# The first mixer of a two-block transformer kernel: products of the next heads traced in steps of six between steps of scores

## The chip, the cores and the metric

The kernel runs on one core of one Trainium2 chip. The metric is the device time of one execution in microseconds (us). The engines are named as in the profile: PE (TensorE's matmuls), PEld (its weight loads), DVE (VectorE), ACT (ScalarE), POOL (GpSimd) and SP (SyncE, which issues most DMAs).

## The reference, cut to what matters

The program computes two blocks one after the other. The change lies in the first layer of block 2, in the mixer that stands ahead of that layer's feed-forward part. It works on 512 tokens of `x` and 256 context tokens, 768 in all, each 1024 wide:

```python
def mixer_ab(hx, hc, w_in, w_out, sink, lam_vec, subln_g, lam_init, tab, ctx_queries):
    p = hx @ w_in                                   # q, k, v of both kinds of heads
    ...                                             # axial rotary embedding of qa, ka, qb, kb
    pc = hc @ w_in
    ...
    oa = window_gqa_latent(qa, ka, va, cka, cva, sink)          # 8 heads, window and context
    ob = from_blocks(lax.map(lambda qblk: diff_attend(qblk, [(kb, vb), (ckb, cvb)], lam),
                             to_blocks(qb)))                     # 4 heads, two softmaxes each
    yx = jnp.concatenate([oa, diff_out(ob, subln_g, lam_init)], axis=-1) @ w_out
    ...                                             # the same for the 256 context tokens

def diff_attend(q, kv_parts, lam):
    ...
    outs = [jnp.einsum('bhqk,bkhd->bqhd', (p[:, 0] - lam * p[:, 1]).astype(v.dtype), v)
            for p, (_, v) in zip(probs, kv_parts)]
```

The windowed heads see their neighbouring tiles of 128 keys and the context. A differential head takes two softmaxes over all 768 keys and subtracts the second, scaled by `lam`, from the first.

## The kernel before, in words

All large products are done as three matmuls each (`mm3`, lines L207 to L209): an operand is split in a high and a low part, and high by high, high by low and low by high are summed in PSUM. A product of one weight tile of 128 columns with the 768 tokens ("load" of q, k or of a pair of windowed queries) is 24 matmuls of 512 columns and 24 of 256. It then goes through `rope_sink`: ACT copies it out of PSUM (L1280), DVE, POOL and DVE rotate it (L1281 to L1284), ACT and DVE write its halves (L1286, L1287, for the last 256 tokens L259 and L260), and `queries` or `keys` move halves between partitions by DMAs issued by SP (L1306). ACT also writes a twin of one half (L1277, L1289). A load of v (`values`, L1470 on) has three sets of 48 matmuls of 256 columns.

In `mixer0` two kinds of units follow each other. Wa, Wb, Wc with a number are the three parts (token tiles 0 and 1, 2 and 3, context) of a pair of windowed heads; Dx and Dc with a number are the two parts (four token tiles, two context tiles) of a differential head. A unit has a generator of scores and one of weighing. The scores of a Dx tile are two rows of 512 and 256 columns (`scores_64`, L1333 and L1334), one for each softmax, each in one of the two PSUM buffers "s2". DVE takes the maximum (L1504), ACT the exponentials and their sum (L1506), DVE its reciprocal (L1507), POOL scales the first (L1510), and DVE joins the two (L1512). Weighing transposes the probabilities by matmuls with the identity (L1347 for D, L700 for W), splits them into halves (ACT L256 and DVE L257, for W L703 and L705) and multiplies them with the values; the D units then normalise with two more transposes (L1533 to L1548).

`unit` weaves the scores of a unit with the weighing of the unit before it, one step by one. The order of units and loads is the table `SEQ`. A load in it is traced whole, between two units; a "." finishes the weighing of the unit before at that point. From the trace a list scheduler makes each engine's order, so the order of instructions is near to that of the program, and not the same. PSUM has eight banks: two buffers "t" (transposes), two "s2" of two banks, one "o" (weighing), one "g" (loads; head 0's q and k use "t").

Of the kernel before, what the change touches and what calls it, by code (L numbers as in the profile page):

```python
# [1363 lines left out]
class Win:  # L1364
# [91 lines left out]
class Diff:  # L1456
# [4 lines left out]
    def load(self, hF, win, h, what, tag="g"):  # L1461

        K, P = self.K, self.P
        c, scale = (512, 0.125) if what == "q" else (1280, 1.0)
        s = (Halves(K, P, P.t("ds", [128, 768], K_DS, F32R)) if what == "q" else
             Halves(K, P, P.t("kl", [128, 768], 1, F32R), P.t("kl1", [128, 768], 1, F32R)))
        gemm_F(K, hF, win[:, :, c:c + 512], 768, lambda j, o, p: s.sink(P, scale)(o, p), [h], tag=tag)
        self.qk[what, h] = s.queries() if what == "q" else s.keys()

    def values(self, hF, win, h, order=(0, 2, 4), early=False):  # L1470
# [595 lines left out]
def hF_tile(P, n=768):  # L2066
# [1 line left out]


STEP = 1.0  # L2070
SEQ = ("k0 Wq0 q0 Wa0 Dx0 Dc0 q1 k1 Wb0 Dx1 Dc1 Wc0 Wq1 Wa1 q2 k2 Wb1 v2 Dx2 . Wc1 Wq2 Dc2 . Wa2 q3 Wb2 k3 Wc2 Dx3 . Wq3 Wa3 Wb3 "
       "Wc3 Dc3")
CTX_FIRST = (4, 5, 0, 1, 2, 3)
PARTS = ((512, 768), (0, 256), (256, 512))

# [1 line left out]
def mixer0(K, hF, finish):  # L2077
# [6 lines left out]
    with ExitStack() as es:  # L2084
# [54 lines left out]
        def diff(h, tiles):
            unit("diff", lambda probs: df.scores(h, tiles, probs), lambda probs: df.weigh(h, tiles, probs), 4 + h if tiles[0] else None)  # L2140

        def qk(h, *what):
            for x in what:
                if x == "v":
                    run_all(df.values(hF, win, h))
                else:
                    df.load(hF, win, h, x, "g" if h else "t")

        for what in SEQ.split():
            if what == ".":  # L2150
                weigh_last()
                continue
            x, h = what[:-1], int(what[-1])
            if x == "Wq":
                W.load_q(hF, win, h)
            elif x in ("Wa", "Wb", "Wc"):
                units = units if x > "Wa" else list(W.units(h))
                unit("win", *units["abc".index(x[1])], h if x == "Wc" else None)
            elif x in ("Dx", "Dc"):
                diff(h, (0, 1, 2, 3) if x == "Dx" else (4, 5))  # L2160
# [171 lines left out]
```

## Time and profile before

| | us |
|---|---|
| median of three runs | 2549.37 |
| lowest and highest | 2546.64 to 2550.6 |
| profiled execution | 2548.71 |
| its span | 2546.7 |
| mean granted clock of PE, share of full speed | 0.982 |
| the mixer of the change in the span | some 850 to 1164 |

Busy time is the time in which an engine has an instruction under way; matmuls overlap in the records, so PE at 100% in a window is a continuous stream. In a timeline a row has its start, its length, the engine, the line and the operation, and in brackets the idle time ahead of it with the instruction that ended it. Places are named by their time in the span.

### The profile page before, as it was taken

How to read it: one execution, taken by the hardware profiler on the slowest of the kernel's cores; microseconds unless marked ns; L12 is line 12 of the kernel's file. 1: busy time of each engine (PE TensorE's matmuls, PEld its weight loads, DVE VectorE, ACT ScalarE, POOL GpSimd, SP SyncE). 2: the span in 40 equal slices, each digit the busy share in tenths (PEclk: the TensorE clock that was granted, in tenths of full speed). 3: DMA queues.
4: the chain of work that ended last, by engine and by line, in shares of the span. 5: the costliest groups of instructions: out<-in, count | busy, mean ns of one | idle time of the engine just before them, and what ended most of it. 6: DMA issues, size and time to landing. Idle time of an engine off the chain costs nothing. (4 is left out here: it accounts for less than half of the span.)

```text
span 2546.7 us, 37857 instructions
## 1 busy us (share of the span) xinstructions
PE 2417.0 (95%) x15436; PEld 1980.4 (78%) x15436; DVE 1199.3 (47%) x2075; ACT 996.9 (39%) x1802; POOL 303.4 (12%) x393
## 2 busy tenths in 40 slices
PE   8999989999999988989899999999899999999998
PEld 6567758788887867768888888888777768888886
DVE  5654474433446575763532223233756564423344
ACT  4642244432325454553522211212555564432222
POOL 1101132000001122220200000000232222000001
PEclk9999989999999999989999999999999999999999
DMA  8765475333334312122411222222331124333332
GB/s 271 243 199 170 162 262 178 92 99 91 99 100 148 85 51 60 50 90 83 150 58 59 66 67 62 64 83 62 109 74 35 40 67 126 106 99 99 93 106 91
DMA packets 251005, 270.74 MB, mean 106 GB/s; under 512 B 23744, under 2 KB 198256, under 8 KB 244688
## 3 DMA queue, kind: packets, MB, share of 16 engines
q1 hardware_dynamic: 249600, 264.00, 33.6%
q0 software_dynamic: 1232, 4.33, 0.5%
q8 instruction: 121, 1.98, 0.3%
q14 instruction: 52, 0.43, 0.1%
HBM read 231.90 MB, written 25.45 MB: 101 GB/s over the span
## 5 line engine op out<-in xcount | busy, mean ns | idle before, releaser
L207 PE MATMUL ps<-hFh,wh 128*128 128x512 f32 (+1 forms) x1752 | 629.0, 360 | 11.0 <-ACT qk_l L1277 3.5
L208 PE MATMUL ps<-hFl,wh 128*128 128x512 f32 (+1 forms) x1752 | 625.0, 357 | 1.5 <-DVE hFl L266 1.3
L200 DVE TENSOR_TENSOR wl<-wr,wh 128x1024 fp32r<-128x1024 f32 (+3 forms) x258 | 307.3, 1192 | 672.5 <-ACT wh L199 655.4
L209 PE MATMUL ps<-hFh,wl 128*128 128x512 f32 (+1 forms) x1752 | 623.5, 356 | 0.5 <-DVE wl L200 0.5
L199 ACT CAST wh<-wr 128x1024 fp32r<-128x1024 f32 (+3 forms) x258 | 263.2, 1021 | 711.9 <-PE ps L208 350.5
L207 PEld LDWEIGHTS ps<-hFh,wh 128*128 128x128 f32 x1752 | 332.7, 190 | 76.4 <-issue 14.5
L209 PEld LDWEIGHTS ps<-hFh,wl 128*128 128x128 f32 x1752 | 333.0, 190 | 53.5 <-issue 5.6
L208 PEld LDWEIGHTS ps<-hFl,wh 128*128 128x128 f32 x1752 | 333.5, 190 | 48.9 <-DVE hFl L266 3.1
L207 PE MATMUL ps<-wh,h_h 128*128 128x512 f32 x590 | 229.7, 389 | 0.7 <-ACT wh L199 0.7
L208 PE MATMUL ps<-wl,h_h 128*128 128x512 f32 x590 | 229.7, 389 | 0.0
L209 PE MATMUL ps<-wh,h_l 128*128 128x512 f32 x590 | 229.5, 389 | 0.0
L1827 POOL TENSOR_TENSOR yg<-y,gainrow 128x512 f32<-128x512 f32 x28 | 38.7, 1384 | 1316.2 <-DVE y L1119 866.5
L207 PEld LDWEIGHTS ps<-wh,h_h 128*128 128x128 f32 x590 | 110.8, 188 | 24.0 <-ACT wh L199 1.1
L208 PEld LDWEIGHTS ps<-wl,h_h 128*128 128x128 f32 x590 | 110.8, 188 | 23.0 <-DVE wl L200 0.2
L209 PEld LDWEIGHTS ps<-wh,h_l 128*128 128x128 f32 x590 | 110.8, 188 | 23.0
L1238 DVE TENSOR_TENSOR hraw<-hraw,ps 128x512 f32<-128x512 f32 (+1 forms) x70 | 40.1, 573 | 176.0 <-PE ps L209 176.0
L1628 DVE TENSOR_REDUCE sm<-ps 128x1 f32<-128x768 f32 x64 | 60.9, 952 | 49.3 <-PE ps L209 48.6
L265 ACT CAST h_h<-hraw 128x512 fp32r<-128x512 f32 (+1 forms) x70 | 36.9, 527 | 120.4 <-DVE hraw L1238 120.4
L207 PE MATMUL ps<-wh,hFh 128*128 128x256 f32 (+2 forms) x256 | 80.3, 315 | 1.2 <-DVE qk_l L257 1.2
L208 PE MATMUL ps<-wl,hFh 128*128 128x256 f32 (+2 forms) x256 | 80.2, 313 | 0.2 <-DVE wl L200 0.2
L209 PE MATMUL ps<-wh,hFl 128*128 128x256 f32 (+2 forms) x256 | 80.2, 313 | 0.0
L1632 POOL TENSOR_SCALAR ms<-ms,sm 128x768 f32<-128x768 f32 x64 | 62.0, 970 | 149.1 <-DVE sm L1631 145.6
(643 smaller groups left out, 4174.8 us busy)
## 6 DMA issues: line engine op xcount, KB each, us to landing
wr<-in_ffn_w_dram SPq DMA_DIRECT2D x126, 512.0 KB, 3.8
aw<-in_ada_w_dram SPq DMA_DIRECT2D x48, 1024.0 KB, 5.1
wr<-in_mlp_w_dram SPq DMA_DIRECT2D x60, 512.0 KB, 3.9
wr<-in_w_in_dram SPq DMA_DIRECT2D x25, 512.0 KB, 6.1
x<-xr SPq DMA_DIRECT2D x20, 512.0 KB, 2.8
xr<-x SPq DMA_DIRECT2D x18, 512.0 KB, 3.7
wr<-in_ab_w_in_dram SPq DMA_DIRECT2D x16, 512.0 KB, 4.3
wr<-in_w_out_dram SPq DMA_DIRECT2D x8, 512.0 KB, 4.5
```

Source lines behind the costliest of these rows:

```text
L199: nc.scalar.copy(dst(hi), view(raw))
L200: nc.vector.tensor_tensor(out=dst(lo), in0=view(raw), in1=dst(hi).bitcast(F32), op=SUB)
L207: mm(out, a.hi, b.hi, start=start, stop=False)
L208: mm(out, a.hi, b.lo, start=False, stop=False)
L209: mm(out, a.lo, b.hi, start=False, stop=stop)
L265: nc.scalar.copy(s.hi, x)
L1238: v.tensor_tensor(out=raw[:, c], in0=raw[:, c], in1=p, op=MUL)
L1628: v.tensor_reduce(out=mx, in_=p[:, 0:768], axis=AX.X, op=MAX, negate=True)
L1632: nc.gpsimd.tensor_scalar(out=s, in0=s, scalar1=r, scalar2=1.0, op0=MUL, op1=MUL)
L1827: nc.gpsimd.tensor_tensor(out=t[:, h[0]], in0=y[:, h[0]], in1=g[:, h[0]], op=MUL)
```

## The change: what it does

The loads become generators. `load_steps` yields after every six matmuls (eight steps for a load), `values` after every twelve. One background generator, `loading`, runs through the loads in the order of `LOADS`; `weave` advances it by `SHARES` steps at each score step of a unit (one in the W units, two in D, three in Wb2 and Wc2). `ready` runs what is still missing ahead of a unit that needs it. The units have a regular order, three W and two D for each number. The points at which a weighing was finished early are gone, and all loads use the bank "g".

The core of the diff (left out: the empty lines, and the code that reads the tables):

```diff
+def load_steps(K, act, src, sink, tag):
+
+    w = K.weight(src)
+    for o, e in ((0, 512), (512, 768)):
+        p = K.ps(tag)[:, 0:e - o]
+        for k in range(8):
+            K.mm3(p, w[:, k], act[:, k, o:e], k == 0, k == 7)
+            if k % 2 and k < 7:
+                yield
+        sink(o, p)
+        if not o:
+            yield
...
-        gemm_F(K, hF, win[:, :, c:c + 512], 768, lambda j, o, p: s.sink(P, scale)(o, p), [h], tag=tag)
+        yield from load_steps(K, hF, win[:, :, c + 128 * h:c + 128 * h + 128], s.sink(P, scale), tag)
...
-SEQ = ("k0 Wq0 q0 Wa0 Dx0 Dc0 q1 k1 Wb0 Dx1 Dc1 Wc0 Wq1 Wa1 q2 k2 Wb1 v2 Dx2 . Wc1 Wq2 Dc2 . Wa2 q3 Wb2 k3 Wc2 Dx3 . Wq3 Wa3 Wb3 "
-       "Wc3 Dc3")
+SHARES = {"Wa": 1, "Wb": 1, "Wc": 1, "Dx": 2, "Dc": 2, "Wb2": 3, "Wc2": 3}
+UNITS = ("Wa0 Wb0 Wc0 Dx0 Dc0 Wa1 Wb1 Wc1 Dx1 Dc1 Wa2 Wb2 Wc2 Dx2 Dc2 Wa3 Wb3 Wc3 Dx3 Dc3").split()
+LOADS = ("Wq0 q0 k0 Wq1 q1 k1 Wq2 q2 v2 k2 Wq3 q3 k3").split()
+NEEDS = {"W": ("Wq",), "D": ("q", "k", "v")}
...
+        def loading():
+            while loads:
+                yield from loads[0][1]
+                loads.pop(0)
+                yield
...
         def unit(name, scores, weigh, sent=None):
             probs = []
-            weave(marked(K, name, scores(probs)), (going[0] if going else iter(()), STEP))
+            weave(marked(K, name, scores(probs)), (going[0] if going else iter(()), STEP), (bg, SHARES.get(name, SHARES[name[:-1]])))
             weigh_last()
```

The instructions are the same in number on PE; they move. Three places show it on PE. In these rows a name is followed by its number in the program; the changed kernel's lines L1347, L1348, L1361, L714 and L728 are L1333, L1334, L1347, L700 and L714 of the kernel before.

The first place is the mixer's first scores. Of the kernel before, the end of the third load and the first rows of Wa0's scores (ps_7985 and ps_7999); ps_7955 is the second part of that load:

```order
L207 MATMUL ps_7955<-hFh_6980,wh_7916 128x256
L208 MATMUL ps_7955<-hFl_6981,wh_7916 128x256
L209 MATMUL ps_7955<-hFh_6980,wl_7917 128x256
L1333 MATMUL ps_7985<-qk_h_7323,qk_h_7838 128x256
L1334 MATMUL ps_7985<-qk_h_7321,qk_h_7838 128x256
L1333 MATMUL ps_7985<-qk_h_7323,qk_h_7838 128x256
L1334 MATMUL ps_7985<-qk_h_7321,qk_h_7838 128x256
L1333 MATMUL ps_7999<-qk_h_7323,qk_h_7838 128x256
L1334 MATMUL ps_7999<-qk_h_7321,qk_h_7838 128x256
```

Of the changed kernel, the last of the ten matmuls of q0's load (ps_7856) that follow the load Wq0, and the first scores:

```order
L207 MATMUL ps_7856<-hFh_6980,wh_7852 128x512
L208 MATMUL ps_7856<-hFl_6981,wh_7852 128x512
L209 MATMUL ps_7856<-hFh_6980,wl_7853 128x512
L207 MATMUL ps_7856<-hFh_6980,wh_7852 128x512
L1347 MATMUL ps_7833<-qk_h_7323,qk_h_7760 128x256
L1348 MATMUL ps_7833<-qk_h_7321,qk_h_7760 128x256
L1347 MATMUL ps_7833<-qk_h_7323,qk_h_7760 128x256
L1348 MATMUL ps_7833<-qk_h_7321,qk_h_7760 128x256
L1347 MATMUL ps_7863<-qk_h_7323,qk_h_7760 128x256
```

Before, three whole loads stand ahead of the first scores; now one load and ten matmuls of the second.

The second place is Dx0. Of the kernel before, two rows of its scores (ps_8104 and ps_8115) and what lies between them: matmuls of the next load (ps_8333), of Wa0's values (ps_8066) and a transpose:

```order
L1333 MATMUL ps_8104<-qk_h_7761,qk_h_7912 128x512
L1334 MATMUL ps_8104<-kl_7759,qk_h_7912 128x512
L1333 MATMUL ps_8104<-qk_h_7761,qk_h_7912 128x256
L1334 MATMUL ps_8104<-kl_7759,qk_h_7912 128x256
L714 MATMUL ps_8066<-pt_h_8173,wv_7337 64x256 x2
L209 MATMUL ps_8333<-hFh_6980,wl_8330 128x512
L1347 MATMUL ps_8210<-c_ident,pr_8049 128x128
L207 MATMUL ps_8333<-hFh_6980,wh_8329 128x512
L1333 MATMUL ps_8115<-qk_l_7762,qk_l_7913 128x512
L1334 MATMUL ps_8115<-kl_1269_7760,qk_l_7913 128x512
L1333 MATMUL ps_8115<-qk_l_7762,qk_l_7913 128x256
L1334 MATMUL ps_8115<-kl_1269_7760,qk_l_7913 128x256
```

Of the changed kernel, three rows of the same scores (ps_8236, ps_8291, ps_8302) and the first of the next (ps_8349):

```order
L1348 MATMUL ps_8236<-kl_8085,qk_h_7848 128x512
L1347 MATMUL ps_8236<-qk_h_8087,qk_h_7848 128x256
L1348 MATMUL ps_8236<-kl_8085,qk_h_7848 128x256
L1347 MATMUL ps_8291<-qk_h_8087,qk_h_7848 128x512
L1348 MATMUL ps_8291<-kl_8085,qk_h_7848 128x512
L1347 MATMUL ps_8291<-qk_h_8087,qk_h_7848 128x256
L1348 MATMUL ps_8291<-kl_8085,qk_h_7848 128x256
L1347 MATMUL ps_8302<-qk_l_8088,qk_l_7849 128x512
L1348 MATMUL ps_8302<-kl_1340_8086,qk_l_7849 128x512
L1347 MATMUL ps_8302<-qk_l_8088,qk_l_7849 128x256
L1348 MATMUL ps_8302<-kl_1340_8086,qk_l_7849 128x256
L1347 MATMUL ps_8349<-qk_h_8087,qk_h_7848 128x512
```

Between these rows no matmul of a load or of a weighing stands any more; the next load's first four (ps_8475) follow two and a half rows later.

The third place is the end of Dx3's scores. Of the kernel before, the start of Dx3's weighing (ps_10495 and ps_10507 transposes, ps_10494 the product with the values) and Wa3's scores (ps_10662, ps_10676) within it:

```order
L1347 MATMUL ps_10495<-c_ident,pr_10475 128x128
L1347 MATMUL ps_10507<-c_ident,pr_10475 128x128
L207 MATMUL ps_10494<-pt_h_10500,qk_h_9337 128x512
L1333 MATMUL ps_10662<-qk_l_7324,qk_h_10589 128x256
L1334 MATMUL ps_10662<-qk_l_7322,qk_h_10589 128x256
L1333 MATMUL ps_10662<-qk_l_7324,qk_h_10589 128x256
L1334 MATMUL ps_10662<-qk_l_7322,qk_h_10589 128x256
L1333 MATMUL ps_10676<-qk_l_7324,qk_h_10589 128x256
L1334 MATMUL ps_10676<-qk_l_7322,qk_h_10589 128x256
L1333 MATMUL ps_10676<-qk_l_7324,qk_h_10589 128x384
L1334 MATMUL ps_10676<-qk_l_7322,qk_h_10589 128x384
L208 MATMUL ps_10494<-pt_l_10501,qk_h_9337 128x512
```

Of the changed kernel, the last scores of Dc3 (ps_10895, ps_10904) and Dx3's weighing (transposes ps_10883, ps_10916, ps_10928, product ps_10882):

```order
L1347 MATMUL ps_10895<-qk_h_10418,qk_h_10119 128x256
L1348 MATMUL ps_10895<-kl_10416,qk_h_10119 128x256
L1347 MATMUL ps_10904<-qk_l_10419,qk_l_10120 128x256
L1348 MATMUL ps_10904<-kl_1883_10417,qk_l_10120 128x256
L1361 MATMUL ps_10883<-c_ident,pr_10821 128x128
L1361 MATMUL ps_10916<-c_ident,pr_10821 128x128
L207 MATMUL ps_10882<-pt_h_10888,qk_h_9523 128x512
L208 MATMUL ps_10882<-pt_l_10889,qk_h_9523 128x512
L209 MATMUL ps_10882<-pt_h_10888,qk_l_9524 128x512
L207 MATMUL ps_10882<-pt_h_10921,qk_h_9523 128x512
L1361 MATMUL ps_10928<-c_ident,pr_10726 128x128
L1361 MATMUL ps_10928<-c_ident,pr_10759 128x128
```

Dx3 and Dc3 are the last units now: behind these scores only Dx3's and Dc3's weighing stands ahead of the output product. The last load (k3) ends within the scores of Wc3.

## Rows read from the trace of the kernel before

**Rows 1.** The page: busy time of the engines; shares of the chain of waits.
```profile
PE 2417.0 (95%) x15436; PEld 1980.4 (78%) x15436; DVE 1199.3 (47%) x2075; ACT 996.9 (39%) x1802; POOL 303.4 (12%) x393
...
PE 22%; DVE 3%; issue 1%; ACT 1%; DMA 1%; POOL 1%; DVEq 0%; POOLq 0%; ACTq 0%
```

**Rows 2.** Windows: us, PE, PEld, DVE, ACT, POOL busy, PEclk, DMA share, GB/s.
```profile
885.00:925.00 40.00, 37.47 (x216) 30.00 (x215) 30.85 (x70) 24.35 (x52) 11.52 (x17) 0.96 0.13 38
940.00:980.00 40.00, 33.17 (x179) 25.36 (x178) 28.77 (x74) 21.54 (x50) 12.12 (x25) 0.91 0.09 24
1036.00:1076.00 40.00, 36.95 (x224) 29.99 (x223) 31.30 (x86) 23.98 (x55) 15.36 (x30) 1.00 0.18 57
1100.00:1140.00 40.00, 31.28 (x172) 23.94 (x169) 30.93 (x62) 24.15 (x47) 10.27 (x20) 0.87 0.34 112
1157.67:1163.59 5.92, 3.75 (x26) 2.17 (x23) 3.75 (x9) 3.39 (x9) 0.60 (x2) 1.00 0.00 0
1300.00:1350.00 50.00, 50.00 (x290) 44.25 (x289) 13.74 (x18) 11.72 (x18) 0.00 (x0) 1.00 0.21 64
```

**Rows 3.** Waits of PE, 850 to 1165 us: sum, times, longest, all us.
```profile
PE ps L1347 <- DVE pr L1512: 8.2, 5, 3.3
PE ps L1547 <- DVE pt_h L1544: 4.3, 6, 1.1
PE ps L207 <- ACT qk_l L1277: 3.5, 6, 1.1
PE ps L207 <- DVE qk_l L257: 2.1, 3, 1.0
```

**Rows 4.** Timelines, head 0: start us, length us, engine, line, [idle before <-releaser].
```profile
858.29 0.39 PE L209 MATMUL ps<-hFh,wl 128*128 128x512 f32 x1
858.52 0.28 PE L207 MATMUL ps<-hFh,wh 128*128 128x256 f32 x1
864.46 0.42 DVE L260 SCALAR_TENSOR_TENSOR kl<-ps,qk_h 128x256 fp32r<-128x256 f32 x1 [0.37 <-ACT qk_h L259]
880.34 0.35 PE L1333 MATMUL ps<-qk_h,qk_h 128*128 128x256 f32 x1 [1.88 <-ACT qk_h L1286]
```

**Rows 5.** DMA issues, 840 to 1170 us: times, KB, median us to landing.
```profile
qk_h<-ds SPq DMA_DIRECT2D x8, 192.0 KB, 2.8
```

**Rows 6.** Lines by form, 850 to 1165 us: busy us, mean ns, idle before.
```profile
L1504 DVE TENSOR_REDUCE sm<-ps 128x1 f32<-128x768 f32 x32 | 30.2, 949 | 7.7 <-PE ps L1334 7.5
L1512 DVE SCALAR_TENSOR_TENSOR pr<-ds,sm,pr 128x768 f32<-128x768 f32 x16 | 16.3, 1018 | 0.3 <-POOL pr L1510 0.2
L1506 ACT ACTIVATE ds<-ps,sm 128x768 f32<-128x768 f32 x16 | 14.5, 904 | 1.8 <-DVE sm L1504 1.3 <-DVE sm L1507 0.2 <-issue 0.2
L256 ACT CAST pt_h<-ps 128x512 fp32r<-128x512 f32 x28 | 15.8, 587 | 15.9 <-PE ps L1347 15.8
L257 DVE TENSOR_TENSOR pt_l<-ps,pt_h 128x512 fp32r<-128x512 f32 x28 | 18.6, 686 | 6.9 <-ACT pt_h L256 6.8
```

**Rows 7.** Timeline of PE, a row of Dx1's scores.
```profile
953.15 0.50 PE L1333 MATMUL ps<-qk_h,qk_h 128*128 128x512 f32 x1 [1.22 <-ACT pr L1506]
```

**Rows 8.** Timeline of PE, end of Dx3's scores, and Dx3's weighing.
```profile
1125.07 0.69 PE L1347 MATMUL ps<-c_ident,pr 128*128 128x128 f32 x2 [3.33 <-DVE pr L1512]
1130.36 1.04 PE L1347 MATMUL ps<-c_ident,pr 128*128 128x128 f32 x8
```

**Rows 9.** Timelines of ACT and PE, Dx3's weighing and the mixer's end.
```profile
1137.20 0.59 ACT L1533 COPY pt_h<-ps 128x512 f32<-128x512 f32 x1 [0.98 <-PE ps L209]
1143.82 0.67 ACT L1548 ACTIVATE mo<-ps,sub 128x512 f32<-128x512 f32 x1
1157.39 0.28 PE L1334 MATMUL ps<-kl,qk_l 128*128 128x256 f32 x1
1158.90 0.65 PE L714 MATMUL ps<-pt_l,wv 128*64 128x256 f32 x4 [0.54 <-DVE pt_l L705]
1163.59 0.36 PE L207 MATMUL ps<-wh,hFh 128*128 128x256 f32 x1
```

More of the change, by code (lines that the diff above doesn't have):

```diff
@@ L1397, in load_q @@
         s = Halves(self.K, self.P, self.P.t("ds", [128, 768], K_DS, F32R))
-        gemm_F(self.K, hF, win[:, :, 0:512], 768, lambda _, o, p: s.sink(self.P, 0.125)(o, p), [j], tag=tag)
+        yield from load_steps(self.K, hF, win[:, :, 128 * j:128 * j + 128], s.sink(self.P, 0.125), tag)
         self.q[j] = s.queries()
@@ L1484, in values @@
                     K.mm3(p[:, 256 * ii:256 * ii + 256], hF[:, k, c:c + 128], ws[k // kn][:, k % kn], k == 0, k == 7)
+                    if not early and k in (3, 7) and (ii, k) != (1, 7):
+                        yield
             for b in range(2):
@@ L2107, in mixer0, with load, ready @@
         last, going = [], []
+        def load(what):
+            x, h = what[:-1], int(what[-1])
+            if x == "Wq":
+                yield from W.load_q(hF, win, h)
+            elif x == "v":
+                yield from df.values(hF, win, h)
+            else:
+                yield from df.load(hF, win, h, x)
+        loads = [(x, load(x)) for x in LOADS]
+        def loading():
+            while loads:
+                yield from loads[0][1]
+                loads.pop(0)
+                yield
+        bg = loading()
+        def ready(names):
+            while any(x in names for x, _ in loads):
+                next(bg, None)
         def unit(name, scores, weigh, sent=None):
             probs = []
-            weave(marked(K, name, scores(probs)), (going[0] if going else iter(()), STEP))
+            weave(marked(K, name, scores(probs)), (going[0] if going else iter(()), STEP), (bg, SHARES.get(name, SHARES[name[:-1]])))
             weigh_last()
@@ L2137, in weigh_last @@
                 split_sb(K, mixs[0][:, j], done[j])
[L2139 to L2152, printed above, removed]
-            x, h = what[:-1], int(what[-1])
[L2154 to L2160, printed above, removed]
-            else:
-                qk(h, x)
+        for what in UNITS:
+            x, h = what[:-1], int(what[-1])
+            ready([n + str(h) for n in NEEDS[x[0]]] + (["v2"] if x[0] == "D" and h == 3 else []))
+            if x[0] == "W":
+                if x == "Wa":
+                    units = list(W.units(h))
+                unit(what, *units["abc".index(x[1])], h if x == "Wc" else None)
+            else:
+                tiles = (0, 1, 2, 3) if x == "Dx" else (4, 5)
+                unit(what, lambda probs: df.scores(h, tiles, probs), lambda probs, h=h, tiles=tiles: df.weigh(h, tiles, probs),
+                     4 + h if x == "Dc" else None)
         weigh_last()
```

## The prediction

> **What bounds the kernel now.** I read the busy times first: PE is busy 95% of the span, DVE 47% [rows 1]. The chain of waits comes next, but its shares by engine add up to only some 29% of the span [rows 1], so it doesn't tell what a change in one stage is worth. For that I take windows. In the feed-forward part after the mixer PE is busy 50.00 of 50 us [rows 2]: there nothing waits, so what the mixer loses or saves on PE shifts all the rest by the same amount. Inside the mixer PE isn't always the limit. I took a stretch of 40 us around each Dx's scores [rows 2]. Around Dx1 (940 to 980) PE is busy 33.17 us and the clock averages 0.91; around Dx3 (1100 to 1140) 31.28 and 0.87; around Dx0 and Dx2 it is 37.47 and 36.95 with 0.96 and 1.00. In the list of PE's waits the largest is the one for DVE's joining of the two softmaxes, 8.2 us in 5 waits [rows 3]; one of Dx3's is 3.33 us [rows 8]. In the two quiet stretches loads stand between the rows of the scores (second place of the change). So the question is where after the change PE has something else to do while DVE and ACT work through a D unit.
>
> **Part A, the start.** Before, three loads stand ahead of Wa0's scores, which still wait 1.88 us for the queries' evacuation [rows 4]. Now it is one load and ten matmuls (first place of the change). A 512-column matmul takes 0.23 us from start to start (858.52 less 858.29, rows 4), a 256-column one half of it, so a load is 24 x 0.23 + 24 x 0.12 = 8.4 us. The first load's evacuation ends with DVE's instruction at 864.46 + 0.42 = 864.9 [rows 4]; then SP moves halves by DMA, 2.8 us to landing [rows 5], and with 0.5 us for issue and release, my estimate, the scores start at 868.2. The load's 24 shorter matmuls begin at 858.52, so PE ends it at 861.4 and, with ten more (2.3 us), is done at 863.7. It stands for 4.5 us, 2.6 more than before. Bounds: nothing, if another load's matmuls slip in, to 4.5.
>
> **Part B, the D units' scores.** DVE needs for one Dx tile two reductions of 0.949 and a joining of 1.018 us [rows 6], 2.9, and three short operations between; I take 3.0. PE needs two rows of 0.70 (512 and 256 columns twice: 2 x 0.23 + 2 x 0.12). There are two buffers, so a row waits until ACT has read the row two before it: the wait of 1.22 us for L1506 in Dx1 is that [rows 7]. Counted from row 1's end, row 8 can start after two tiles on DVE (6.0), and of the third two reductions and an exponential (2 x 0.95 + 0.9 = 2.8, rows 6), and ends 0.7 later: 9.5 us, in which PE has seven rows, 4.9. A bare Dx so loses 4.6 us. Now what stands between: by the changed order, Dx0 has four load matmuls ahead of its last row (0.9 us), Dx1 sixteen and eight of 256 columns (2.8), Dx2 eleven of 512 (2.5), Dx3 none, since k3 ends in Wc3. That leaves 3.7 + 1.8 + 2.1 + 4.6 = 12.2 us of standing. To it comes the clock. Before, the four stretches lose, as time without work and as clock (40 us times what is missing to 1.00): Dx0 2.5 + 1.6, Dx1 6.8 + 3.6, Dx2 3.1 + 0, Dx3 8.7 + 5.2 [rows 2], together 31.5. Not all of it is the D scores' own: half of what the quiet stretches lose on average, 1.8 us, I put down to other waits in each, an estimate, so 24.3 remain. A real stall paid 4.4 for the clock (the mean of 3.6 and 5.2). I give the two barest, Dx0 and Dx3, 4.4 each, and 1 to each of the others: 12.2 + 10.8 = 23.0 against 24.3, so -1.3. The stalls change places; the sum stays. Bounds: -10, if Dx1 and Dx2 are covered fully and Dx0 nearly, to +8, if all four pay the clock and only the surplus over the quiet stretches (17.1) was the scores' before.
>
> The Trainium skill (Perfetto Trace Analysis, section Optimization Strategy) says that regimes with different contended engines may gain by being interleaved. The trace bears it out where loads lie between D rows, as in Dx0 of before. By that rule the 24.3 us would go; it is rival 1. The rule needs work on PE to interleave, and at Dx3 the order shows none.
>
> **Part C, the end.** Before, Dx3's weighing lay among Wa3's and the following scores: from the last joined tile (1125.07, rows 8) to its normalised output (1143.82, rows 9). Behind the last score, at 1157.39, the next stage's first product starts at 1163.59 [rows 9]; of the 5.92 us between the end and that start PE is busy 3.75 [rows 2]. Now Dx3's and Dc3's weighing stand alone there (third place). Its six steps each pass through ACT's copy of 0.587 and DVE's difference of 0.686 us [rows 6]: 6 x 1.3 = 7.8, as the two transposing buffers keep PE only that far ahead. The normalisation took 6.6 us from its copy at 1137.20 to 1143.82 [rows 9], beside other work; alone I take 4.6. Then Dc3's own chain, 6.2 as before. That is 18.6 against 5.9, 12.7 more. Not all is lost: work came along that PE did elsewhere before. Of Dx3's weighing 18 products of 0.23 (4.1) and 24 transposes at 0.10 (eight start to start in 0.79 after 1130.36, rows 8; 2.4): 6.5. Out of the end went Wc3's last products and transposes, about 1.0 by the row of four at 1158.90 [rows 9]. And one wait of 1.1 us in the normalisation [rows 3] isn't met elsewhere any more. 12.7 - 6.5 + 1.0 - 1.1 = +6.1. Bounds: +3, if the steps overlap as they do among scores, to +9, if the clock falls there and the output product starts at the lower one.
>
> **Part D, the bank of the loads.** All loads share one PSUM bank, and PE waited for its evacuation 3.5 us in 6 waits for ACT and 2.1 in 3 for DVE [rows 3]. With score steps between the sets I take half: -2.8. Bounds: -5.6 to +3, the latter if head 0's q and k, which used the two transposing buffers, now wait as the others do.
>
> The Trainium skill (Perfetto Trace Analysis, section Optimizing Tensor Performance) wants independent groups of matmuls to rotate through PSUM banks, so that one's evacuation lies beside the next. One bank for all 25 sets goes against it. By the rule each set would wait some 0.6 us, 15 us in all; the trace shows 5.6, since other work already lies between most sets, and I stay with the rows.
>
> The order keeps PE's number of instructions, and DMAs and casts of weights are the same; they come with the loads that they belong to, and SP's moves of q and k with them. In the rows of PE's waits none is for weights, so I cost that at nothing; a weight that came late would cost about two operations of the size of DVE's joining, 2 us, once.
>
> **Sum.** 2.6 - 1.3 + 6.1 - 2.8 = +4.6 on the profiled execution's 2548.71 (span 2546.7) gives 2553.3; the median of the runs lies 0.7 higher. I predict 2554.
>
> **Rivals.**
> 1. *Interleaving works.* Loads in steps of six go wherever PE waits, and the D stalls vanish: -24.3 + 2.6 + 6.1 - 2.8 = -18.4, or 2530. For it: the quiet stretches of before. Against it: the scheduler has taken the six-step pieces out of the first rows of Dx0 again (second place), and Dx3 has no load left.
> 2. *The trades cancel.* Dx1 and Dx2, with loads at hand, lose nothing (1.8 + 2.1 + 2 for the clock less), and the normalisation overlaps (C at +3, 3.1 less): 4.6 - 5.9 - 3.1 = -4.4, or 2544. For it: both units have loads ahead of their first rows. Against it: DVE's pace of 3.0 us a tile holds for the last four rows too, where few stand.
> 3. *Each Dx costs what before's Dx1 and Dx3 did*, 10.4 and 13.9 less 1.8, on average 10.35; four of them 41.4 against 24.3, with A, C and D +17.1 + 5.9 = +23: 2572. It is slower by PE's standing for DVE's joining (L1361 in the new lines), and the half clock after it, in every head. It decides if the loads beside Dx1 and Dx2 cover less than half of their 4.6 us. Against it: twenty-four short and eleven long matmuls stand there.
> 4. *The change doesn't do what it says*, the scheduler putting the loads together again: 2549. The second load of head 3 does stand nearly whole ahead of Dx2; most others don't.
>
> **How the numbers follow.** Forecast: 0.37. Rivals 1 to 4: 0.17, 0.2, 0.2 and 0.06. A difference of 0.2%, 5 us, is what a measurement can tell from none. Faster by more holds rival 1 and half of rival 2: 0.27. Within it: the other half, rival 4 and half of the forecast: 0.34. Slower: the other half and rival 3: 0.39. The range takes in some of rival 1 and of rival 3, each spread by 5 us or so around its number: 2532 to 2570 leaves out about 0.1 on either side. The forecast's own range is 2549 to 2559.
>
> **What would show it.** In the changed profile the mixer's windows show PE under 34 of 40 us around Dx0 and Dx3, with a lower clock behind; the first scores wait 4 to 5 us for a DMA from SP; the last score and the output product lie 17 to 20 us apart instead of 6.2; waits for the evacuation of loads sum to 2 to 4 us. If no stretch of 40 lies under 36, rival 1 is right; if all four lie under 33.5, rival 3. I would be wrong above all if what the schedule orders and what PE waits for differ: loads that run ahead of the scores fill no stall behind them.

## The result, and the profile after

| | before | changed |
|---|---|---|
| median, us (4 runs each, one chip) | 2549.98 | 2573.56 |
| range, us | 2546.64 to 2550.73 | 2570.20 to 2575.45 |
| ratio to before | 1 | 1.0088, 95% interval 1.0073 to 1.0103 |
| span of the profiled execution, us | 2546.7 | 2573.7 |
| the mixer: last product ahead of its loads to the output's first product, us | 310.8 | 337.7 |

The change makes the kernel slower by 0.88% by the ratio of the runs, some 23 us. The forecast was 2554 with a range of 2532 to 2570, so the time lies outside, at rival 3's number. The mixer accounts for all of it: it is 26.9 us longer and the span 27.0. Its length is taken from the last product of the first values to the output's first product. These are the two mixers as windows, the kernel before and the changed one, columns as in [rows 2]:

```profile
852.83:1163.59 310.76, 274.62 (x1666) 221.03 (x1664) 206.72 (x510) 170.05 (x367) 86.37 (x136) 0.96 0.24 66
854.07:1191.73 337.66, 284.97 (x1666) 228.43 (x1664) 210.03 (x510) 168.85 (x367) 87.47 (x128) 0.93 0.22 61
```

PE runs 1666 matmuls in both. Of the 26.9 us, 16.55 are more time in which it has no matmul under way (52.69 us instead of 36.14), and 10.35 are the same matmuls taking longer at a lower granted clock (0.93 instead of 0.96).

The next windows are those of the changed kernel: the start, 40 us around Dx0, Dx1, Dx2 and Dx3, each from 3 us ahead of that unit's first long row, and the end:

```profile
854.07:886.00 31.93, 25.80 (x140) 21.98 (x138) 14.20 (x38) 10.78 (x22) 7.30 (x7) 0.89 0.26 66
907.93:947.93 40.00, 34.04 (x171) 26.83 (x168) 27.62 (x59) 19.04 (x41) 10.67 (x19) 0.91 0.28 72
977.80:1017.80 40.00, 35.89 (x197) 28.14 (x194) 28.66 (x58) 19.62 (x43) 10.10 (x19) 0.96 0.27 72
1076.21:1116.21 40.00, 34.44 (x178) 27.93 (x176) 27.80 (x58) 19.91 (x42) 11.38 (x19) 0.91 0.17 45
1140.45:1180.45 40.00, 28.78 (x127) 19.17 (x126) 29.61 (x63) 22.56 (x48) 6.87 (x10) 0.83 0.25 74
1169.80:1191.73 21.93, 15.52 (x59) 10.40 (x58) 8.44 (x18) 7.27 (x15) 2.31 (x4) 0.73 0.00 0
```

In the kernel before, the window of [rows 2] for Dx0 starts 2.6 us ahead of the first long row and the one for Dx3 1.6 us behind it, but the one for Dx1 starts 7.2 us behind, and the one for Dx2 (1036 to 1076) lies nearly all behind its scores, whose long rows start from 1012.86 to 1039.30. So for Dx1 and Dx2 of before these windows, from 3 us ahead of the first long row, are used in their place:

```profile
929.77:969.77 40.00, 33.71 (x180) 25.20 (x180) 29.89 (x75) 22.91 (x53) 12.95 (x24) 0.91 0.23 62
1009.86:1049.86 40.00, 37.31 (x261) 32.62 (x260) 23.58 (x53) 18.02 (x39) 8.45 (x12) 1.00 0.18 50
```

With the prediction's own measure (time without work, and the clock's part) the four stretches of the changed kernel lose 6.0 + 3.6, 4.1 + 1.6, 5.6 + 3.6 and 11.2 + 6.8 us, together 42.5. Before it was 4.1, 9.9, 2.7 and 13.9, together 30.6. Dx1 became better, the other three worse. The start, not among these stretches, loses 6.1 us without work and 3.5 of clock.

PE's waits in the mixer of the changed kernel, columns as in [rows 3]; L1347 is now the score's matmul, L1291 the twin's evacuation (L1277 before):

```profile
PE ps L1347 <- ACT pr L1523: 13.5, 6, 4.5
PE ps L1564 <- DVE pt_h L1561: 7.8, 6, 3.4
PE ps L1347 <- ACT ds L1523: 7.4, 9, 1.6
PE ps L207 <- ACT qk_l L1291: 7.4, 3, 3.5
PE ps L207 <- DVE qk_l L257: 2.5, 2, 1.9
PE ps L207 <- ACT rx L1294: 1.8, 4, 0.7
PE ps L1361 <- DVE pr L1529: 0.3, 2, 0.2
```

Of the kernel before, three lines that [rows 3] doesn't show:

```profile
PE ps L1333 <- ACT pr L1506: 2.9, 4, 1.2
PE ps L1333 <- ACT ds L1506: 2.1, 4, 1.0
PE ps L207 <- ACT rx L1280: 0.7, 1, 0.7
```

Two things are new. The wait for DVE's joining (L1361) fell from 8.2 us to 0.3, but the scores' waits for ACT's exponentials grew to 13.5 and 7.4 us, where before they were 2.9, 2.1 and 0.8 (the last for the context tiles). Together these are 21.2 us instead of 14.0. And the loads' waits for their bank (L207 for ACT's twin, for DVE's half and for ACT's copy) are 7.4, 2.5 and 1.8 us, together 11.7, instead of 3.5, 2.1 and 0.7, together 6.3. Two of them are long.

The first of these two stands at the mixer's start, in PE's timeline:

```profile
856.22 0.47 PE L207 MATMUL ps<-hFh,wh 128*128 128x512 f32 x1 [1.88 <-DVE qk_l L257]
...
865.54 0.28 PE L209 MATMUL ps<-hFh,wl 128*128 128x256 f32 x1
...
869.28 0.79 PE L207 MATMUL ps<-hFh,wh 128*128 128x512 f32 x1 [3.46 <-ACT qk_l L1291]
...
873.71 0.41 PE L1347 MATMUL ps<-qk_h,qk_h 128*128 128x256 f32 x1
```

The first load waits 1.88 us for DVE to have read the values (v) out of the bank, and 0.68 us more between its two sets, for ACT's copy. Its last matmul starts at 865.54; the next load could start 0.12 us later and starts at 869.28, because ACT's evacuation of the bank isn't done. The three waits are 6.0 us, all but 0.1 of the time without work at the start. Before, PE has no idle time between 852.83 and 878, while the three loads of head 0 run in turn from the banks "t" and "g". Behind the long wait a 512-column matmul takes 0.43 us from start to start instead of 0.23, until about 875. The scores that I had expected to wait (873.71) don't wait at all; behind the ten matmuls at half clock the queries are there. What ACT did in that time:

```profile
862.07 0.59 ACT L1294 COPY rx<-ps 128x512 f32<-128x512 f32 x1 [6.46 <-PE ps L209]
...
866.06 0.63 ACT L1300 ACTIVATE qk_h<-rx 128x512 fp32r<-128x512 f32 x1 [3.40 <-DVE rx L1298]
...
867.78 1.04 ACT L199 CAST wh<-wr 128x1024 fp32r<-128x1024 f32 x1
...
868.85 0.38 ACT L1291 ACTIVATE qk_l<-ps 64x256 fp32r<-64x256 f32 x1
```

ACT copies the first 512 columns at 862.07, then waits 3.40 us for the rotation that goes through DVE, POOL and DVE. The second set was finished on PE at about 865.7, but its evacuation comes behind the rotated halves: L259 starts at 867.37, and the twin (L1291) comes behind a weight's cast of 1.04 us as well. The bank is free at 869.2.

The end, in PE's timeline: the last score, and the second transposes of Dx3's normalisation:

```profile
1169.80 0.42 PE L1348 MATMUL ps<-kl,qk_l 128*128 128x256 f32 x1
...
1186.07 1.12 PE L1564 MATMUL ps<-c_ident,pt_h 128*128 128x128 f32 x4 [3.44 <-DVE pt_h L1561]
```

21.9 us lie between the last score and the output's product (1191.73) instead of 6.2, with a granted clock of 0.73 in it. In the kernel before no wait of the normalisation is over 1.1 us [rows 3]: there other work lay beside it.

### The profile page after: what moved, and what is told of

Its sections match the earlier page's. It is cut to its first block, busy times and chain, and to the rows that moved or that the text cites. A ratio compares the mean times of both kernels' runs of the same rounds, so it can differ in the third digit from the quotient of the medians.

```text
span 2573.7 us, 37857 instructions
## 1 busy us (share of the span) xinstructions
PE 2423.1 (94%) x15436; PEld 1983.8 (77%) x15436; DVE 1202.7 (47%) x2075; ACT 995.6 (39%) x1802; POOL 306.3 (12%) x393
## 3 DMA queue, kind: packets, MB, share of 16 engines
q8 instruction: 121, 1.98, 0.3%
## 5 line engine op out<-in xcount | busy, mean ns | idle before, releaser
L207 PE MATMUL ps<-hFh,wh 128*128 128x512 f32 (+1 forms) x1752 | 631.3, 361 | 16.5 <-ACT qk_l L1291 7.4
L207 PEld LDWEIGHTS ps<-hFh,wh 128*128 128x128 f32 x1752 | 332.2, 190 | 84.1 <-issue 14.7
L207 PE MATMUL ps<-wh,h_h 128*128 128x512 f32 x590 | 229.7, 389 | 0.3 <-ACT wh L199 0.3
L207 PEld LDWEIGHTS ps<-wh,h_h 128*128 128x128 f32 x590 | 110.8, 188 | 23.6 <-ACT wh L199 0.7
L265 ACT CAST h_h<-hraw 128x512 fp32r<-128x512 f32 (+1 forms) x70 | 36.9, 527 | 121.3 <-DVE hraw L1252 121.3
L207 PE MATMUL ps<-wh,hFh 128*128 128x256 f32 (+2 forms) x256 | 80.9, 318 | 0.0
```

The lines of the kernel that those rows point to most:

```text
L207: mm(out, a.hi, b.hi, start=start, stop=False)
L265: nc.scalar.copy(s.hi, x)
```

## The experiments

Each kernel's ratio is to runs of the kernel before on the same chip. "Mixer" is its length as above, in its profiled execution.

| kernel | what it is | median, us | ratio, interval | mixer, us |
|---|---|---|---|---|
| changed | | 2573.56 | 1.0088 (1.0073 to 1.0103) | 337.7 |
| e1_tail | changed, Dx3 ahead of W3 | 2566.51 | 1.0071 (1.0051 to 1.0090) | 327.9 |
| e2_start | changed, head 0's loads whole, as before | 2558.93 | 1.0044 (1.0030 to 1.0058) | 323.3 |
| e4_units | before, order of units and loads alone | 2565.85 | 1.0067 (1.0045 to 1.0090) | 327.9 |
| e5_steps | changed, order of units and loads as before | 2551.52 | 1.0013 (1.0000 to 1.0025) | 316.8 |
| e3_freeg | changed, bank copied out by DVE | 2561.66 | 1.0051 (1.0033 to 1.0069) | 322.9 |
| e11_start_g | e2_start with one bank | 2576.79 | 1.0108 (1.0092 to 1.0124) | 341.3 |
| e8_start_tail | e1 and e2 together | 2554.40 | 1.0021 (1.0006 to 1.0036) | 316.4 |
| e6_before_freeg | before, bank copied out | 2536.49 | 0.9948 (0.9933 to 0.9964) | 297.6 |
| e9_start_tail_freeg | e8 with the copy | 2537.68 | 0.9961 (0.9948 to 0.9973) | 303.1 |
| e10_steps_freeg | e5 with the copy | 2530.43 | 0.9934 (0.9912 to 0.9955) | 295.2 |

**e1_tail**

```diff
-UNITS = ("... Wa3 Wb3 Wc3 Dx3 Dc3").split()
-LOADS = ("Wq0 q0 k0 Wq1 q1 k1 Wq2 q2 v2 k2 Wq3 q3 k3").split()
+UNITS = ("... Dx3 Wa3 Wb3 Wc3 Dc3").split()
+LOADS = ("Wq0 q0 k0 Wq1 q1 k1 Wq2 q2 v2 k2 q3 k3 Wq3").split()
```

> The changed kernel with Dx3 put ahead of Wa3, Wb3, Wc3 (as the kernel before has it) and q3, k3 loaded ahead of Wq3; everything else as changed. Theory (the end): in the changed kernel 21.9 us lie between the last score and the output product, since Dx3's weighing stands alone there, against 6.2 before. With W3's scores beside it these should be 6 to 7 again, 15 less, of which some 6.5 come back as work elsewhere; Wq3's load now lies beside Dx3's scores and saves some 3. Expected 2560 to 2564 against 2573.6. Rival (the steps themselves cost, wherever they stand, because PE changes between kinds of matmuls): within 3 us of 2573.

Measured: 1.0071. The mixer is 9.8 us shorter; by the runs' ratio it is 4 us, and the two intervals overlap. The 21.9 us at the end became 8.4, so that the end is dear is shown in the mixer; how much of it comes back elsewhere isn't the same in both measures. The saving beside Dx3 didn't come: the last of Dx3's rows waits for an exponential, and Wa3's first scores wait for the move of their queries, as PE's timeline of e1_tail shows:

```profile
1137.55 0.50 PE L1347 MATMUL ps<-qk_l,qk_l 128*128 128x512 f32 x1 [2.50 <-ACT ds L1523]
...
1143.39 0.55 PE L1347 MATMUL ps<-qk_l,qk_h 128*128 128x256 f32 x1 [2.21 <-DMA qk_h<-ds]
```

Wq3, laid beside Dx3, is the load that the next unit needs. Its rotation and its move by DMA come late.

**e2_start**

```diff
-SHARES = {"Wa": 1, "Wb": 1, "Wc": 1, "Dx": 2, "Dc": 2, "Wb2": 3, "Wc2": 3}
-LOADS = ("Wq0 q0 k0 Wq1 q1 k1 Wq2 q2 v2 k2 Wq3 q3 k3").split()
+SHARES = {"Wa": 1, "Wb": 1, "Wc": 1, "Dx": 2, "Dc": 2, "Wa0": 0, "Wb0": 0, "Wc0": 0, "Wb2": 3, "Wc2": 3}
+LOADS = ("k0 Wq0 q0 Wq1 q1 k1 Wq2 q2 v2 k2 Wq3 q3 k3").split()
...
-                yield from df.load(hF, win, h, x)
+                yield from df.load(hF, win, h, x, "g" if h else "t")
+        ready(("k0", "Wq0", "q0"))
         for what in UNITS:
```

> The changed kernel with head 0's loads k0, Wq0, q0 traced whole ahead of Wa0, q0 and k0 in the two transposing banks, as before; no steps beside Wa0, Wb0, Wc0. Theory (one bank for loads): the changed kernel waits 1.9, 0.7 and 3.5 us at its first load's bank and then runs some 6 us at half clock, 9.6 us lost up to 886 us against 3.5 before; with the old start 6 us come back: 2567. Less is gained if Dx0, with fewer loads near it, waits longer. Rival (the start costs nothing in the end, since the scores of head 0 then wait for DVE anyway): 2573, no change.

Measured: 1.0044, half of the loss gone. The mixer is 14.4 us shorter, twice what I expected. In the timelines Dx0's first long row starts 45.7 us after the mixer's beginning instead of 56.9, and its last 61.1 instead of 78.1. So 11.2 us are won ahead of Dx0 and 5.8 within its rows, where Wq1's second part now lies behind the fifth, sixth and seventh row. Some 2 of these 17 us are lost again by Dx1, and from there the two kernels run nearly in step (Dx3's last long row at 295.1 and 310.1 us).

**e11_start_g**: e2_start with all three loads in the bank "g".

> As e2_start (head 0's loads k0, Wq0, q0 whole ahead of Wa0, no steps beside W0), but all three in the one bank of the loads instead of two of them in the transposing banks. Theory (the bank makes the start dear): the 3.5 us waits and the half clock stand between the loads again, 8 to 10 us more than e2_start: 2567. Rival (what e2_start gained came from the loads being whole and ahead, with Wq1 beside Dx0): within 3 of e2_start's 2559.

Measured: 1.0108, 0.64% above e2_start; the mixer is 18.0 us longer. It is even slower than the changed kernel. The waits for the bank are 10.5 us in 3, against 3.6 in 1 of e2_start. PE's waits of e11_start_g and of e2_start, the same line of each:

```profile
PE ps L207 <- ACT qk_l L1291: 10.5, 3, 3.5
```

```profile
PE ps L207 <- ACT qk_l L1291: 3.6, 1, 3.6
```

The two kernels differ in the bank alone, so the bank is what makes the start dear in this order, and the rival, as it was stated, falls. Something of it stays: Dx0's rows, from the first long one to the last, take 16.7 us here, with Wq1 beside them, against 21.2 in the changed kernel. The first score starts 38.4 us after the mixer's beginning instead of 27.5. A further 4.4 us come before Dx0: a wait of 2.00 us of the windowed heads' scores for DVE, and more of the matmuls standing ahead of Dx0 (140 instead of 115).

**e3_freeg**

```diff
         if o >= 512:
-            evac_split(K, s[:, o:o + n], p, scale)
+            x = P.t("rx", [128, 512], 2)[:m, :n]
+            v.tensor_copy(x, p)
+            p = x
+            evac_split(K, s[:, o:o + n], p, scale)
```

> The changed kernel with one instruction more in a load: DVE copies the last 256 tokens out of the loads' bank at once, and ACT and DVE read the copy; so the bank is free before ACT has gone through the rotation of the first 512. Theory (one bank, held until ACT has done the rotation and a cast): the two waits of 3.5 us for the twin's evacuation (before head 0's second load, before Dx2's) fall under 1 us and the half clock after each goes: 8 to 12 us less, 2562 to 2566 against 2573.6. Rival (the next wait comes at once: the scores need those queries and PE waits for them instead): 2570 to 2575.

Measured: 1.0051; 0.37% less by the ratios, 9.5 us, and the mixer is 14.8 us shorter. But the gain isn't the one that the theory wanted. The wait at the start only falls from 3.46 to 1.98 us, now for DVE's copy, which on DVE comes behind the rotation of the first 512:

```profile
867.52 0.51 PE L207 MATMUL ps<-hFh,wh 128*128 128x512 f32 x1 [1.98 <-DVE rx L1290]
```

Of PE's waits in e3_freeg (lines from the rotation on are three later than in the changed kernel):

```profile
PE ps L1350 <- ACT pr L1526: 5.4, 8, 1.1
PE ps L207 <- DVE rx L1290: 4.9, 5, 2.0
PE ps L207 <- ACT rx L1297: 4.3, 7, 1.0
```

With 1.9 us for DVE's half the loads' waits for their bank are 11.1 us in all, against 11.7 without the copy: none is long any more, but there are more of them. What falls are the scores' waits for exponentials, to 5.4, 4.0 and 1.9 us (the last for the context tiles), 11.3 instead of 20.9. And it isn't the start that gains: Dx0's first long row is at 55.7 us, only 1.2 earlier. The gain comes head by head (Dx1 at 122.0 instead of 126.7, Dx2 at 215.7 instead of 225.1, Dx3 at 276.5 instead of 289.4). The evacuations of loads stand on ACT and DVE ahead of those exponentials, but the copy also changes the scheduler's order, and the two aren't separated.

**e4_units**: the kernel before with this table.

```diff
-SEQ = ("k0 Wq0 q0 Wa0 Dx0 Dc0 q1 k1 Wb0 Dx1 Dc1 Wc0 Wq1 Wa1 q2 k2 Wb1 v2 Dx2 . Wc1 Wq2 Dc2 . Wa2 q3 Wb2 k3 Wc2 Dx3 . Wq3 Wa3 Wb3 "
-       "Wc3 Dc3")
+SEQ = ("k0 Wq0 q0 Wa0 Wb0 Wc0 Dx0 Dc0 Wq1 q1 k1 Wa1 Wb1 Wc1 Dx1 Dc1 Wq2 q2 v2 k2 Wa2 Wb2 Wc2 Dx2 Dc2 Wq3 q3 k3 Wa3 Wb3 Wc3 "
+       "Dx3 Dc3")
```

> The order of units alone: the kernel before with its table of units and loads written in the changed kernel's order, each load traced whole ahead of its head's units, no steps. Theory (the order of the units costs, the steps don't): Dx3 at the end costs its 10 to 12 us as in the changed kernel, three loads one behind the other in one bank cost 3.5 us and half clock per pair, and no load lies beside any Dx: 2575 to 2590. Rival (the steps cost): near before, 2550 to 2560.

Measured: 1.0067, mixer 327.9 us. Below both ends that I gave the theory and above the rival's. The order of units and loads alone costs 17.1 us in the mixer, with the same 22.0 us at the end as the changed kernel. e2_start has this order and these banks too, and the steps: its mixer is 4.6 us shorter (1.0044 against 1.0067; the intervals overlap). So the steps by themselves cost nothing in this order. The whole splits up in three: 17.1 us for the order, 4.6 less with the steps, and 14.4 more with head 0's loads in steps and in one bank make the 26.9.

**e5_steps**

```diff
-SHARES = {"Wa": 1, "Wb": 1, "Wc": 1, "Dx": 2, "Dc": 2, "Wb2": 3, "Wc2": 3}
-UNITS = ("Wa0 Wb0 Wc0 Dx0 Dc0 Wa1 ...
-LOADS = ("Wq0 q0 k0 Wq1 q1 k1 Wq2 q2 v2 k2 Wq3 q3 k3").split()
+SHARES = {"Wa": 0, "Wb": 0, "Wc": 0, "Dx": 0, "Dc": 0, "Wb0": 4, "Dx1": 2, "Wa1": 2, "Wb1": 3, "Wc1": 2, "Wa2": 2, "Wb2": 2, "Dx3": 2}
+UNITS = ("Wa0 Dx0 Dc0 Wb0 Dx1 Dc1 Wc0 Wa1 Wb1 Dx2 . Wc1 Dc2 . Wa2 Wb2 Wc2 Dx3 . Wa3 Wb3 Wc3 Dc3").split()
+LOADS = ("k0 Wq0 q0 q1 k1 Wq1 q2 k2 v2 Wq2 q3 k3 Wq3").split()
+        ready(("k0", "Wq0", "q0"))
```

> The steps alone: the changed kernel's generators, but units and loads in the order of the kernel before, head 0's loads whole as before; the steps lie beside Wb0 (q1, k1), Dx1 (Wq1), Wa1 (q2), Wb1 (k2, a part of v2), Wc1 (Wq2), Wa2 (q3), Wb2 (k3) and Dx3 (Wq3). Theory (the steps cost nothing, and cover DVE's work where they stand beside D scores): the 10.4 and 13.9 us lost around Dx1 and Dx3 fall by half: 2538 to 2546 against 2550. Rival (the steps cost by themselves): slower than before by 10 or more. Rival (the list scheduler moves them away again): 2550.

Measured: 1.0013, slower by 3 us or equal; the gain didn't come, nor the loss of 10 that the rival wanted. It lies near the last rival's 2550, and the timeline of the kernel before may say why so little changes: there the scheduler had already put the loads that the table has behind Dx1 and Dx3 among their rows. From Dx3's first long row to its last, 17 matmuls of 512 and 24 of 256 columns of Wq3's load lie there, and as many of Wq1's at Dx1. In e5_steps Wq3's load lies beside Dx3 too: its fifth row waits 0.49 us, and the sixth and seventh don't wait. Then it comes back:

```profile
1125.20 0.50 PE L1347 MATMUL ps<-qk_l,qk_l 128*128 128x512 f32 x1 [3.19 <-ACT ds L1523]
...
1131.02 0.55 PE L1347 MATMUL ps<-qk_l,qk_h 128*128 128x256 f32 x1 [2.20 <-DMA qk_h<-ds]
```

Row eight waits 3.19 us for the exponential, the joining 1.98, and Wa3's scores 2.20 for the move of Wq3's queries. The last matmul of Wq3's load starts at 1121.30 here, 9.7 us ahead of those scores. In the kernel before it is 12.2 us, by these rows of PE's timeline, a matmul of the load ahead of Dx3's first long row, the load's last and the scores' first:

```profile
1098.10 0.48 PE L207 MATMUL ps<-hFh,wh 128*128 128x512 f32 x1
...
1114.57 0.36 PE L209 MATMUL ps<-hFh,wl 128*128 128x256 f32 x1
...
1126.81 0.41 PE L1333 MATMUL ps<-qk_l,qk_h 128*128 128x256 f32 x1
```

**e8_start_tail**: the edits of e1_tail and e2_start.

> Both undone together: head 0's loads as in e2_start, and Dx3 ahead of Wa3 with q3, k3 loaded ahead of Wq3 as in e1_tail; the regular order of heads 0 to 2 and the steps stay. Theory (start and end are the whole of the loss and add up): in the mixer 26.9 us more than before in the changed kernel, less 14.4 and 9.7, so 2.8 more than before: 2550 to 2553. Rival (heads 1 and 2 lose too, and the gains overlap): 2556 to 2560.

Measured: 1.0021, mixer 316.4 us, 5.6 more than before. Start and end explain 21.3 of the 26.9 us; what is left, 5.6 us, includes a wait of 4.40 us for Wa3's queries:

```profile
1137.09 0.55 PE L1347 MATMUL ps<-qk_l,qk_h 128*128 128x256 f32 x1 [4.40 <-DMA qk_h<-ds]
```

Its profiled execution is 9 us above its median, 5.8 of them ahead of the mixer (it starts at 859.87), so only the mixer's length is used.

**e6_before_freeg**: the copy of e3_freeg in the kernel before.

> The kernel before with DVE's copy out of the loads' bank (as e3_freeg). Theory: before, waits for the bank sum to 6.3 us, no one over 1.1, and no half clock follows them: 2 to 4 us less, 2544 to 2546. Rival (DVE, with 11 copies more, is late where PE waits for it): 2550 or more.

Measured: 0.9948; 13 us faster than before, more than three times what I expected. Of the loads' waits for their bank, 6.3 us before, one is left:

```profile
PE ps L207 <- DVE qk_l L257: 0.5, 1, 0.5
```

The mixer is 13.2 us shorter. PE's time without work in it falls by 8.0 us (269.49 of 297.59 us are busy), 5.8 of them these waits, and the same matmuls take 5.1 us less at a granted clock of 0.97 instead of 0.96. So the clock is a part that I had left out. One thing follows for the change: with the copy in both kernels it costs 25 us (e3_freeg against e6_before_freeg, 1.0051 against 0.9948), as much as without it.

The same kernel on another chip, beside the next but one:

> The kernel before with DVE's copy out of the loads' bank once more, on one chip beside e12_steps_freeg_again, to tell the two apart. If the steps as such neither gain nor lose, both have the same ratio to before within 0.2%, near 0.995.

Measured: 2539.34 us, 0.9954 (0.9939 to 0.9969).

**e9_start_tail_freeg** and **e10_steps_freeg**: e8 and e5 with the copy.

> e8_start_tail with DVE's copy out of the loads' bank: steps and the regular order for heads 0 to 2, head 0's loads whole, Dx3 ahead of W3, and the bank freed early. Theory (bank, start and end are all that the change loses; the steps as such neither gain nor lose): the waits of 3.9 us for the bank and the half clock go, as in the kernel before, which gained 13: near 2540, no better than the kernel before with the copy (2536.5). Rival (interleaving gains once the bank is free): under 2532.

> e5_steps with DVE's copy out of the loads' bank: order of units and loads of the kernel before, in steps, Wq1 beside Dx1, Wq3 beside Dx3. Theory (a load beside Dx covers DVE's work but its queries then come late for the next unit: in e5_steps 2.2 us for the move to Wa3 and 3.2 us for an exponential): 2538 to 2542, not faster than the kernel before with the copy. Rival (the loads in steps hide the D units once the bank is free): under 2532.

Measured: 0.9961 and 0.9934. By the intervals the regular order, with start and end undone and with the copy, is as fast as the kernel before with the copy; its mixer is 5.5 us longer. e10_steps_freeg came out below the theory's 2538 and within the rival's "under 2532", but its interval overlaps that of e6_before_freeg. So it was run once more beside e6's kernel:

> e10_steps_freeg once more, beside the kernel before with the same copy. If the steps gain where they lie beside Dx1 and Dx3 once the bank is free, its ratio is lower by 0.2% or more than that of the other: 0.993 against 0.995. If not, the two are the same.

Measured: 2536.05 us, 0.9942 (0.9925 to 0.9959), against 0.9954 for the other on that chip. The intervals overlap; whether the steps gain a tenth of a per cent stays open. Both beat the kernel before and the changed one.

## Why the prediction was wrong

**Two steps failed, part D (the bank of the loads) and part B (the sum of the stalls stays), by about the same amount.** Part D was put at -2.8 and came out near +9.8; part B was put at -1.3 and came out near +11.8.

**Part D.** I took the waits that before shows, halved them and allowed up to +3. The loads' waits for their bank are 11.7 us now instead of 6.3, and behind the two long ones the half clock takes 2.9 and 1.5 us more (the windows at the end of this text, 5.97 and 3.08 us at 0.51): together 9.8. That the bank does this at head 0 is shown by e11_start_g against e2_start, 16 us by the ratios (0.64%); in the changed kernel itself it is read from the trace, since a run with nothing undone but the banks of head 0's q and k wasn't made. e3_freeg doesn't price the bank: the same copy gains 13 us in the kernel before. At head 0 before had none of these waits, with its loads in alternating banks; a wait that is hidden has no row, and halving the rows that exist says nothing of it. The number could be had from the trace of before: the first load's second set ends on PE at 861.4 [rows 4], and the last read of its bank is ACT's twin:

```profile
865.53 0.38 ACT L1277 ACTIVATE qk_l<-ps 64x256 fp32r<-64x256 f32 x1
```

So a load that must have the same bank couldn't start for 4.5 us. I worked out most of this chain in part A, up to DVE's read at 864.9, and let the scores wait for it; the next load, which stands ahead of them and needs the bank, waits first. The rule of the Trainium skill (Perfetto Trace Analysis, section Optimizing Tensor Performance) that I set aside there, groups of matmuls in rotating banks, is borne out: 3.46 and 3.54 us at two places where two loads meet. (The one bank takes 27 sets by the table, not 25; no term rests on it.) The second is ahead of Dx2:

```profile
1073.56 0.79 PE L207 MATMUL ps<-hFh,wh 128*128 128x512 f32 x1 [3.54 <-ACT qk_l L1291]
```

It may arise since Wb2 and Wc2 take three steps for each of their score steps, so that the end of one load and the start of the next meet there; no run separates this.

**Part B.** Its model of a bare Dx is right in kind, and every size is too low. By PE's timeline it stands in the long rows for exponentials 4.8 us in Dx0, 2.7 in Dx1, 4.0 in Dx2 and 6.4 in Dx3, 17.9 in all, where I had 3.7, 1.8, 2.1 and 4.6, 12.2 in all. The clock takes 15.6 us in the four windows where I had 10.8. By its own condition the upper bound was wrong too: four stalls with the clock are 12.2 + 17.6, less 17.1 is +12.7, not +8.

What failed most is the cover. Loads do lie between the long rows of Dx0, Dx1 and Dx2, 41 or 42 matmuls in each, but in Dx0 37 of the 41 stand ahead of the end of the first two rows, and in Dx2 30 of 41, with the other 11 behind the stalls. Nothing is left for the third row's wait. In Dx1 16 stand just ahead of the third row, and it doesn't wait. The end of Dx0's first two rows and its third row, and then the last matmul ahead of Dx1's third row and that row:

```profile
919.20 0.28 PE L1348 MATMUL ps<-kl,qk_h 128*128 128x256 f32 x1
922.30 0.50 PE L1347 MATMUL ps<-qk_h,qk_h 128*128 128x512 f32 x1 [2.82 <-ACT pr L1523]
...
990.32 0.28 PE L207 MATMUL ps<-hFh,wh 128*128 128x256 f32 x1
990.45 0.40 PE L1347 MATMUL ps<-qk_h,qk_h 128*128 128x512 f32 x1
```

This is the prediction's last sign of being wrong come true: loads that run ahead of the scores fill no stall behind them. The kernel before could have told. Its two quiet stretches have 9 and 14 load matmuls between the long rows, and its two dear ones, Dx1 and Dx3, have 41 each. At Dx3 no row waits over 0.57 us; what is lost lies behind the rows, in waits of 2.42 and 3.33 us for the joining (the second is in [rows 8]). There ACT was splitting the finished heads (L265), so that the last exponential starts at 1121.60, 1.5 us after its maximum was ready:

```profile
1120.86 0.83 ACT L265 CAST hFh<-hFl 128x768 fp32r<-128x768 f32 x1 [0.63 <-DMA hFl<-dmix]
```

In the changed kernel the same splits come ahead of Dx3's first exponential: DVE does its part of two of them (L266) before it takes the maximum of the first row, ACT waits for the maximum, and PE waits 4.48 us:

```profile
1151.64 0.95 DVE L266 TENSOR_TENSOR hFl<-hFl,hFh 128x768 fp32r<-128x768 f32 x1
...
1153.55 0.90 ACT L1523 ACTIVATE pr<-ps,sm 128x768 f32<-128x768 f32 x1 [1.36 <-DVE sm L1521]
...
1154.60 0.50 PE L1347 MATMUL ps<-qk_h,qk_h 128*128 128x512 f32 x1 [4.48 <-ACT pr L1523]
```

**Part A**, +2.6, had the size of its wait nearly right (3.5 against 4.5 us), but by luck: the wait is for another thing, at another instruction, and belongs to part D. The scores themselves wait no more, so the part is -3.5: before, PE is busy 30.17 of 32.05 us at the start with a clock of 0.95, which is 1.88 us for the queries and 1.6 us of clock, by this window of the kernel before:

```profile
852.95:885.00 32.05, 30.17 (x165) 26.16 (x164) 16.08 (x31) 12.48 (x23) 6.05 (x4) 0.95 0.50 122
```

**Part C**, +6.1, was right in its mechanism: 21.9 us between last score and output product where I had worked out 18.6. Undoing it shortened the mixer by 9.8 us in e1_tail and by 6.9 between e2_start and e8_start_tail (0.23% by the ratios, with intervals that overlap). The clock of 0.73 there, which I had put into the bound, is more than enough for the difference to 18.6. As a check on the whole: -3.5, +11.8 and +9.8 for A, B and D leave 8.8 of the 26.9 us for C, within what undoing it gave. This is an estimate, since the windows overlap at some edges.

**The rivals.** Rival 3 gave 2572, the measured number, but not by its mechanism: PE stands for DVE's joining 0.3 us, not in every head, and not all four Dx lose as much as before's two (Dx1 is better than before); the bank, which it left at -2.8, makes up the difference. That its number came out is luck. Rival 1, interleaving, didn't come as a gain: not without the copy (e5_steps 1.0013), and not clearly with it (0.9934 and 0.9942 against 0.9948 and 0.9954). Where load matmuls stand just ahead of a row it waits less (Dx1's third row); that loads lie somewhere between the rows isn't enough.

What stays open: why the copy shortens the waits for exponentials, the last 5.6 us of the mixer in e8_start_tail beyond the wait shown, and whether the steps gain anything.

## What to carry to other kernels

Before loads are moved so that they meet, take the time from the end of a load's matmuls to the end of the last read of its PSUM buffer, and subtract what stands between; a wait that isn't in the trace because two buffers hid it comes up when there is one. If an engine's queue holds that read behind a long rotation, a copy by another engine can free the buffer earlier: in the old order it gave 0.5% here and took the waits from 6.3 to 0.5 us. In the new order the copy itself came behind the rotation on DVE, and the sum of the waits stayed at 11 us. Count as cover for a wait only what the engine's order has just ahead of it, after the work that the wait is for has begun. And work put beside a stall should not be what the very next unit needs, nor be taken from the end, where nothing else covers the last weighing.

## What was not expected

The clock after a stall can cost nearly as much as the stall. Behind the wait of 3.46 us PE ran at half clock (granted 0.51, the lower of its two levels) for 5.97 us, and the 2.9 us of delay that this makes come on top; behind the one of 3.54 us it was 3.08 us, with 1.5 us of delay. Behind the wait of 1.88 us at 856.22 the next matmuls follow at 0.23 us, so that one cost no clock. The granted clock of the two stretches of the changed kernel:

```profile
869.28:875.25 5.97, 5.97 (x18) 5.00 (x18) 1.25 (x2) 0.00 (x0) 0.00 (x0) 0.51 0.58 156
1073.56:1076.64 3.08, 3.08 (x7) 2.47 (x8) 0.00 (x0) 0.00 (x0) 0.00 (x0) 0.51 0.95 251
```
